# Second attention of a two-layer decoder: the low parts of the weights behind the copies of the transposed probabilities, and the last quarter's transposes behind nine products of the output projection

## The chip, the cores and the metric

The kernel runs on one core of a Trainium2 chip. The metric is the device time of one execution in microseconds (us). The kernel before takes 745.67 us, the median of three runs that lie between 745.35 and 746.33.

## The reference, cut to what matters

The program is a decoder trunk with two layers over 256 positions of 1024 numbers, all in float32. Layer 0 has a dilated attention, layer 1 a "forgetting" attention; behind each stands a SwiGLU feed-forward network. Each of the four is added to the residual stream and has an RMS norm ahead of it. The change lies in the second attention and the projection behind it:

```python
def forgetting_mixer(h, w_in, b_f, w_out):
    proj = h @ w_in                                  # 1024 -> 3*1024 + 16 gates
    q, k, v = ...                                    # 16 heads of 64
    c = lax.cumsum(log_sigmoid(proj[..., 3072:] + b_f), axis=1)
    def block(args):                                 # 128 queries at a time
        s = jnp.einsum('bihd,bjhd->bhij', qi, k) * HEAD_DIM ** -0.5
        s = s + ci[..., None] - ck[:, :, None, :]
        s = jnp.where(key_pos[None, :] <= qpos[:, None], s, NEG_INF)
        p = jax.nn.softmax(s, axis=-1)
        return jnp.einsum('bhij,bjhd->bihd', p, vf)
    return o @ w_out
```

## The kernel before, in words

**Products in three matmuls.** A float32 matrix is split into a high part (a copy in a shorter format) and a low part (the difference). Each product of two tiles is three matmuls: high by high, then two with one low part each (`mm3`, lines 198 to 208; a row of the profile shows the first as L202 and the other two as L207). Weights come from HBM as `raw` tiles of 128x1024 in five buffers, two of them to one piece of weights. For each, ScalarE (ACT) copies the high part `wh` (L79), then VectorE (DVE) subtracts for the low part `wl` (L83). When DVE has done so, the `raw` buffer is free, and the SyncE queue (SP) issues the transfer of the `raw` tile five places on. `weights` (line 149) asks for pieces two units ahead of their use.

**The second attention.** The loop over `b_units` (from line 934) takes one projection of 256 columns a round: for each quarter of the heads (four heads) first q, then k, and the v's of three quarters stand ahead of the loop. `due` holds the steps of the attention of a quarter that are hung into later rounds: the scores (`scores_b`) a round after k, the transposes of the probabilities (`trans_b`) one and a half rounds after the scores, between the two halves of that round's projection, and the products with v (`pv_b`) at the end of the same round, followed there by the next quarter's scores. So one round goes: half a projection, transposes of quarter n, the other half, `pv_b` of n, scores of n+1.

`scores_b` writes scores to four PSUM banks. DVE adds the bias and finds the maxima (L876), ACT takes exponentials (L878), DVE the reciprocals of the sums (L883), and both scale the probabilities `p` (L885 on ACT, L886 on DVE). `trans_b` transposes them on TensorE (PE, L298) into two banks `ps_tr` and one `ps_o`, and DVE copies the three to `pt` tiles (L303). `pv_b` needs these copies (L310); its results are split into `oth` (ACT) and `otl` (DVE), the operands of the output projection.

**The output projection.** `out_proj` (line 630) computes two halves of rows, t = 0 and 1. A product here is one of 16 for each t: n (two halves of the columns) by k (eight tiles of 128 rows of `ot`), three matmuls of 512 columns each. The last quarter gives k = 6 and 7, and its transposes and `pv_b` are still in `due` when `out_proj` begins. For t = 0 it makes the products of n = 0 over the first `done` k's, then the transposes, then what remains of these k's for n = 1, then `pv_b`, then the k's that are left.

**What sets the order.** The engines run in the order of their own instruction streams. The order is set by the code's order, by `first()` (a higher priority for the steps of an attention), and by `issue_after`, which puts an instruction behind another in the order. The list `behind` with `release` already does for the rounds 3 and 5 what the change does for others: it keeps low parts back until a given DVE instruction.

Of the kernel before, what the change touches and what calls it, by code (L numbers as in the profile page):

```python
# [19 lines left out]
KT = D // P  # L20
# [11 lines left out]
def trunk(ctx: ExitStack, tc: tile.TileContext, T, out):  # L32
# [10 lines left out]
    def first():  # L43

        return tc.high_priority(offset=300)

    def psum(tag):
        return ps.tile([P, 512], F32, tag=tag, name=f"ps_{tag}", bufs=2)
# [41 lines left out]
    def piece(key, todo=None):  # L90
        if key[0][:2] == "dn" and key[1] == LATE:
            wh, wl = (y.rearrange("p k c -> p (k c)") for y in fm_tile("ot", KT, 1))
        else:
            wh, wl = (wp.tile([P, WIDE], F32R, tag=y, name=y, bufs=4) for y in ("wh", "wl"))
        if key == GATED:
            wh, wl = (y.rearrange("p (k c) -> p k c", k=KT) for y in (wh, wl))
        for c in range(2):
            raw = wp.tile([P, 1024], F32, tag="raw", name="raw", bufs=5)
            u = slice(c * 1024, (c + 1) * 1024)
            nc.sync.dma_start(raw, T[key[0]][key[1]][:, u])  # L100
            view = lambda y, u=u: y[:, u]
            if key == GATED:
                raw = raw.rearrange("p (k c) -> p k c", c=256)
                view = lambda y, c=c: y[:, c * 4:c * 4 + 4, :256]
            cut = lambda after=None, hold=None, raw=raw, view=view: split((wh, wl), view, raw, False, after, hold)
            if todo is None:
                cut()
            else:
                todo.append(cut)
        if key == GATED:  # L110
            cut = lambda after=None, hold=None: split((wh, wl), lambda y: y[:, :, 256:], wf32, False, after, hold)
            todo.append(cut)
        return wh, wl
# [7 lines left out]
    def xt_tile():  # L121
        full = ap.tile([P, KT, 2, S], F32R, tag="xt", name="xt", bufs=1)
        x = XT((full[:, :, 0, :], full[:, :, 1, :]))
        x.full = full
        return x
# [27 lines left out]
    def weights(nm, i, after=None, ahead=AHEAD, hold=None):  # L153

        upto = order.index((nm, i)) + ahead
        while state["next"] <= min(upto, len(order) - 1):
            key = order[state["next"]]
            cuts = []
            ready[key] = piece(key, cuts)
            for cut in cuts:  # L160
                cut(after, hold)
            state["next"] += 1
        return ready.pop((nm, i))
# [46 lines left out]
    def both(pair, *idx):  # L210
        return tuple(x[idx] for x in pair)
# [43 lines left out]
    def v_tile(o=None, r=None):  # L255

        v = ap.tile([P, 512], F32, tag="v", name="v", bufs=7)
        with first():
            if r:
                for t in range(2):  # L260
                    s = slice(t * S, (t + 1) * S)
                    nc.scalar.activation(v[:, s], o[:, s], AF.Copy, scale=r[t])
            elif o is not None:
                nc.scalar.activation(v, o, AF.Copy)
        return v
# [24 lines left out]
    def masked(s, sc, mask):  # L290
        with first():
            nc.vector.scalar_tensor_tensor(s, sc, HD ** -0.5, mask, op0=ALU.mult, op1=ALU.add)

    def transposed(blocks, copy=nc.vector.tensor_copy, tag="tr", home="pt"):

        tr = psum(tag)
        for i, b in enumerate(blocks):
            nc.tensor.transpose(tr[:, i * P:(i + 1) * P], b, ident)  # L298
        n = len(blocks) * P
        bufs, cols = {"pt": (3, 512), "bias": (4, 6 * P)}[home]  # L300
        w = ap.tile([P, cols], F32, tag=home, name="pt", bufs=bufs)
        with first():
            copy(w[:, :n], tr[:, :n])  # L303
        return w

    def pv(o, v, kb, pr, w, n, start, stop):
# [21 lines left out]
    for i, c in enumerate(room):  # L328
        b = 1 + (i > 1)
        n = S + 512  # L330
# [17 lines left out]
    xt = xt_tile()  # L348
# [15 lines left out]
    part = [sums[:, :S], sums[:, S:512], sums[:, 512:], sqs[:, :512], sqs[:, 512:]]  # L364
# [8 lines left out]
    for k in range(KT):  # L373
        if k % 4 == 0:
            w = tuple(wp.tile([P, 2048], F32R, tag=y, name=y, bufs=4) for y in ("wh", "wl"))
# [49 lines left out]
    x = []  # L425

    ot = fm_tile("ot", KT, 1)
# [102 lines left out]
    due = {}  # L530
# [5 lines left out]
    for i, (hq, g, w) in enumerate(a_units):  # L536
# [3 lines left out]
        elif i:  # L540

            wt = weights("a_in", hq * 9 + g * 3 + w, read if i > 4 else None)
# [9 lines left out]
        if i in (24, 31):  # L552
            x.append(hrow("x"))
            t = len(x) - 1
            nc.sync.dma_start(x[t], T["x"][t * P:(t + 1) * P, :])
        if w < 2:
# [4 lines left out]
            if i == 2:  # L561
# [3 lines left out]
                wt = weights("a_in", 1, second)  # L565
# [61 lines left out]
                parts.append(sq(hn[:, s]))  # L627
        return hn, parts

    def out_proj(nm, ot, h, grow, done, banks):  # L630

        ws = [weights(nm, i) for i in range(4)]
        xt = xt_tile()
        res = []

        def part(t, acc, nk):
            last = None
            for n, k in nk:
                c = (k % 2) * D + n * 512
                last = mm3(acc[n], both(ot, ALL, k, slice(t * P, (t + 1) * P)),  # L640
                           both(ws[k // 2], ALL, slice(c, c + 512)), k == 0, k == KT - 1)
            return last

        def cols(ks):
            return [(n, k) for n in range(2) for k in ks]

        for t in range(2):
            acc = [psum(banks[t]) for _ in range(2)]
            if t == 0:

                nk = cols(range(done))
                last = part(t, acc, nk[:done])
                nk = nk[done:]
                per = -(-len(nk) // (len(due) - 1))
                for i in sorted(due):
                    with tc.issue_after(last.ins):
                        for fn, a in due[i]:
                            fn(*a)
                    last = part(t, acc, nk[:per]) or last
                    nk = nk[per:]  # L660
                due.clear()
                part(t, acc, nk)
                last = part(t, acc, cols(range(done, KT)))
            else:
                part(t, acc, cols(range(2)))
                with tc.issue_after(last.ins):
                    part(t, acc, cols(range(2, 6)))
                    norm_t(*res[0], grow, xt, 0)
                    part(t, acc, cols(range(6, KT)))
            res.append(residual(acc, h[t], f"h_{nm}{t}"))  # L670
        return res, xt
# [110 lines left out]
        return res  # L782

    g_f = load_grow(1)
    hs, xt = out_proj("a_out", ot, x, g_f, 6, ("sc", "mm"))
    causal = const("causal", [P, P])
    bf = cst.tile([P, NH], F32, name="bf")
    nc.sync.dma_start(bf, T["bf"].partition_broadcast(P))
# [9 lines left out]
    hs = ffn(0, hs, xt, g_f, mid)  # L798
    xt, g_b = nxt["xt"], nxt["g"]
# [26 lines left out]
    behind = []  # L826
# [27 lines left out]
    ot = fm_tile("ot", KT, 1)  # L854
# [79 lines left out]
    held = None  # L934
    for i, (hq, w) in enumerate(b_units):
        if i < 3:
            continue
        wt = weights("b_in", hq * 3 + w, behind if i in (3, 5) else None, hold=held)
        o = psum("mm")
        if w < 2:  # L940
            for c in range(2):
                proj_feat(xt, wt, o[:, c * S:(c + 1) * S], c)
                if c == 0:
                    for fn, a in due.pop(i - 0.5, ()):
                        fn(*a)
            if w == 0:

                for fn, a in due.pop(i, ()):
                    fn(*a)
            bq[hq][w] = ap.tile([P, 2, S], F32, tag=f"fm{w}", name=f"fb{w}", bufs=2)  # L950
            with first():
                held = nc.scalar.activation(bq[hq][w], o.rearrange("p (a b) -> p a b", a=2), AF.Copy,
                                            scale=(0.125, 1.0)[w])
            if w == 1:
                j = i + 1

                later(j, scores_b, hq)
                if hq < 2:
                    for pr in range(2):
                        later(j + 1, bias, hq + 2, pr)  # L960
                later(j + 1.5, trans_b, hq)
                for pr in range(2):
                    later(j + 2, pv_b, hq, pr)
        else:
            for t in range(2):
                proj_tok(xt, wt, o[:, t * S:(t + 1) * S], t)
                if t == 0:
                    for fn, a in due.pop(i - 0.5, ()):
                        fn(*a)
            bq[hq][w] = v_tile(o)  # L970
        for fn, a in due.pop(i, ()):
            fn(*a)
    g_f = load_grow(3)
    hs, xt = out_proj("b_out", ot, [h for h, _ in hs], g_f, 5, ("mm", "sc"))

    def finish(t, h, parts):
        r = rstd(parts)
# [10 lines left out]
    hs = ffn(1, hs, xt, g_f, mid)  # L988
    acc, h1 = hs[1]
# [3 lines left out]
    for o, (a, b) in zip(acc, ((0, 512), (512, 256), (768, 256))):  # L993
# [4 lines left out]
        else:  # L998
            parts.append(ap.tile([P, 1], F32, tag="ssq", name="ssq", bufs=8))
            last = nc.vector.scalar_tensor_tensor(psum("sc")[:, :b], hn[:, s], 1.0 / D, hn[:, s], op0=ALU.mult,  # L1000
                                                  op1=ALU.mult, accum_out=parts[-1])
# [104 lines left out]
```

## Time and profile before

| | |
|---|---|
| time, median of three runs | 745.67 us (745.35 to 746.33) |
| profiled execution: its own time / its span from first to last instruction | 749.27 us / 747.5 us |
| clock granted to PE, mean over the span | 0.994 |
| busy: PE / PE's weight loads | 737.5 us / 680.5 us |
| busy: DVE / ACT / POOL | 492.6 / 375.7 / 66.8 us |
| moved from and to HBM | 136.07 MB read, 1.07 MB written |

The page names engines by PE (matmul), PEld (its weight loads), DVE, ACT, POOL (GpSimd) and SPq (the queue of SyncE, which issues transfers). A row of a timeline has the start in us from the span's beginning, a length in us, the engine, the line of the kernel, the operation, what it writes and reads, a shape and a count; idle time ahead of it and what ended that stand in brackets. Where a count is above one, the row covers several instructions in succession. Lengths of matmuls overlap, since they are pipelined: what a matmul costs is read from start to start.

### The profile page before, as it was taken

What the parts mean: (1) busy time and instruction counts of PE and PEld (TensorE: products, weight loads), DVE (VectorE), ACT (ScalarE), POOL (GpSimd) and SP (SyncE); (2) the same over time, 40 slices, a digit from 0 to 9 for tenths busy, and PEclk for the clock granted to TensorE, in tenths of its full rate; (3) what the DMA queues carried; (4) which work ended last, traced back from release to release, by engine and by line L of the source; (5) the groups of instructions that cost most, each with busy time, mean ns of one, the idle gap of its engine ahead of it and who ended that gap; (6) DMA issues with size and microseconds to landing.
All of it is one profiled execution on the core that took longest, in us unless ns stands there. A gap on an engine that the chain in (4) does not pass through costs nothing.

```text
span 747.5 us, 14342 instructions
## 1 busy us (share of the span) xinstructions
PE 737.5 (99%) x5916; PEld 680.5 (91%) x5916; DVE 492.6 (66%) x768; ACT 375.7 (50%) x617; POOL 66.8 (9%) x98
## 2 busy tenths in 40 slices
PE   9999999999999999999999999999999999999996
PEld 7999989999988789999999988979789999999995
DVE  6997987787888575545455474686767545456533
ACT  7536437437436565344454453576555444444521
POOL 0600003005005000000000004211000000000001
PEclk9999999999999999999999999999999999999998
DMA  8865544644646267565667452874537665656601
GB/s 330 298 203 171 177 155 151 203 159 153 209 144 222 82 229 238 191 200 179 202 204 241 138 168 87 288 243 146 171 105 221 231 198 180 202 189 215 209 1 56
DMA packets 39441, 138.07 MB, mean 185 GB/s; under 512 B 4528, under 2 KB 5840, under 8 KB 39376
## 3 DMA queue, kind: packets, MB, share of 16 engines
q1 hardware_dynamic: 39232, 137.01, 55.3%
q8 instruction: 46, 0.75, 0.4%
q14 instruction: 19, 0.16, 0.1%
q10 hardware_dynamic: 144, 0.15, 0.1%
HBM read 136.07 MB, written 1.07 MB: 183 GB/s over the span
## 4 chain that ended last, share of the span: by engine, by line
PE 90%; ACT 3%; DMA 3%; DVE 2%; issue 1%; SPq 0%; POOL 0%; POOLq 0%; DVEq 0%; ACTq 0%
PE ps_mm L207 31%; PE ps_mm L202 16%; PE ps_tr L207 9%; PE ps_sc L207 8%; PE ps_o L207 7%; PE ps_tr L202 5%; PE ps_sc L202 4%; PE ps_o L202 4%; PE ps_o L310 2%; DMA raw<-in_b_in 2%; DVE wl L83 1%; DMA otl<-in_lead 1%; PE ps_tr L298 1%; ACT wh L79 1%; PE ps_sc L473 1%; ACT p L878 1%
## 5 line engine op out<-in xcount | busy, mean ns | idle before, releaser
L79 ACT ACTIVATE wh<-raw 128x1024 fp32r<-128x1024 f32 x236 | 243.2, 1055 | 240.4 <-PE ps_tr L207 66.5
L83 DVE TENSOR_TENSOR wl<-raw,wh 128x1024 fp32r<-128x1024 f32 x236 | 288.5, 1242 | 88.1 <-ACT wh L79 87.8
L202 PE MATMUL ps_mm<-xt,wh 128*128 128x256 f32 x816 | 228.2, 280 | 0.0
L207 PE MATMUL ps_mm<-xt,wl 128*128 128x256 f32 x816 | 226.8, 278 | 0.1
L207 PE MATMUL ps_mm<-xt,wh 128*128 128x256 f32 x816 | 226.6, 278 | 0.0
L202 PEld LDWEIGHTS ps_mm<-xt,wh 128*128 128x128 f32 x816 | 153.9, 189 | 1.8 <-issue 1.7
L207 PEld LDWEIGHTS ps_mm<-xt,wl 128*128 128x128 f32 x816 | 153.4, 188 | 0.5 <-DVE wl L83 0.5
L207 PEld LDWEIGHTS ps_mm<-xt,wh 128*128 128x128 f32 x816 | 153.4, 188 | 0.0
L207 PE MATMUL ps_tr<-xt,wl 128*128 128x256 f32 x304 | 83.8, 276 | 0.0
L207 PE MATMUL ps_tr<-xt,wh 128*128 128x256 f32 x304 | 83.8, 276 | 0.0
L202 PE MATMUL ps_tr<-xt,wh 128*128 128x256 f32 x304 | 83.6, 276 | 0.0
L702 DVE TENSOR_TENSOR sa<-ps_tr,sa 128x256 f32<-128x256 f32 x38 | 16.1, 424 | 73.9 <-PE ps_tr L207 73.8
L207 PEld LDWEIGHTS ps_tr<-xt,wh 128*128 128x128 f32 x304 | 57.1, 188 | 0.0
L207 PEld LDWEIGHTS ps_tr<-xt,wl 128*128 128x128 f32 x304 | 57.1, 188 | 0.0
L202 PEld LDWEIGHTS ps_tr<-xt,wh 128*128 128x128 f32 x304 | 56.9, 188 | 0.0
L284 POOL COPY v<-v 32x256 f32<-32x256 f32 x64 | 38.0, 594 | 176.1 <-ACT v L280 173.4
L202 PE MATMUL ps_mm<-wh,xt 128*128 128x512 f32 (+1 forms) x144 | 49.8, 346 | 0.0
L207 PE MATMUL ps_mm<-wl,xt 128*128 128x512 f32 (+1 forms) x149 | 49.1, 335 | 0.0
L207 PE MATMUL ps_mm<-wh,xt 128*128 128x512 f32 (+1 forms) x149 | 49.1, 335 | 0.0
L172 POOL TENSOR_SCALAR rs<-ssq 128x1 f32<-128x1 f32 x7 | 2.1, 303 | 422.8 <-ACT junk L181 422.8
L202 PE MATMUL ps_sc<-wh,ah 128*128 128x512 f32 x80 | 31.4, 392 | 0.0
L207 PE MATMUL ps_sc<-wl,ah 128*128 128x512 f32 (+1 forms) x82 | 31.3, 385 | 0.0
(230 smaller groups left out, 1103.3 us busy)
## 6 DMA issues: line engine op xcount, KB each, us to landing
raw<-in_gu SPq DMA_DIRECT2D x88, 512.0 KB, 4.8
raw<-in_a_in SPq DMA_DIRECT2D x68, 512.0 KB, 4.6
raw<-in_dn SPq DMA_DIRECT2D x44, 512.0 KB, 4.6
raw<-in_b_in SPq DMA_DIRECT2D x24, 512.0 KB, 4.7
raw<-in_a_out SPq DMA_DIRECT2D x8, 512.0 KB, 5.3
raw<-in_b_out SPq DMA_DIRECT2D x8, 512.0 KB, 4.9
bias<-sums SPq DMA_DIRECT2D x8, 384.0 KB, 6.1
grow<-in_norms SPq DMA_DIRECT2D x4, 512.0 KB, 5.9
```

The source lines that it names most:

```text
L79: a = nc.scalar.activation(view(hi), src, AF.Copy)
L83: return nc.vector.tensor_tensor(view(lo), src, view(hi).bitcast(F32), op=ALU.subtract)
L172: nc.gpsimd.tensor_scalar(m, s, rest, None, op0=ALU.add)
L202: nc.tensor.matmul(o, sh, mh, start=start, stop=False)
L207: last = nc.tensor.matmul(o[:, u], s, m[:, u], start=False, stop=end and u.stop == n)
L284: nc.gpsimd.tensor_copy(v[1 + a % 2][n:n + 32, a // 2 * S:a // 2 * S + S], by_t[a * 32:a * 32 + 32, t, g])
L298: nc.tensor.transpose(tr[:, i * P:(i + 1) * P], b, ident)
L310: nc.tensor.matmul(o[h * HD:(h + 1) * HD], v[:, c:c + HD], w(h), start=start, stop=stop)
L473: nc.tensor.matmul(sc[h][c, o:o + 64], q[HR[h], pr, qb * P + a * 32:qb * P + a * 32 + 32], k[HR[h], pr].rearrange("p (b n) -> p b n", b=2) ...
L702: nc.vector.tensor_tensor(a, u, sg, op=ALU.mult)
L878: nc.scalar.activation(s[:, u], s[:, u], AF.Exp, bias=nm[:, j:j + 1], scale=-1.0, accum_out=den[:, j:j + 1])
```

## The change

Two things are changed. In rounds where transposes are due (7, 9 and 11), the low parts of the weights that the round asks for are kept in a list `lows` and are put behind the last copy of the transposed probabilities (`copied["last"]`) in DVE's order. And `out_proj` has two numbers in the place of one: `ks`, the k's that are ready ahead of the last quarter (6 in both attentions; for the second it was 5), and `done`, the products ahead of the first step that is due (9 for the second attention, where it was 5). For the first attention both are 6, which is what was there.

```diff
+    copied = {}
+
     def transposed(blocks, copy=nc.vector.tensor_copy, tag="tr", home="pt"):
...
-            copy(w[:, :n], tr[:, :n])
+            copied["last"] = copy(w[:, :n], tr[:, :n])
...
-    def out_proj(nm, ot, h, grow, done, banks):
+    def out_proj(nm, ot, h, grow, ks, done, banks):
...
-                nk = cols(range(done))
+                nk = cols(range(ks))
                 last = part(t, acc, nk[:done])
                 nk = nk[done:]
...
-                last = part(t, acc, cols(range(done, KT)))
+                last = part(t, acc, cols(range(ks, KT)))
...
-        wt = weights("b_in", hq * 3 + w, behind if i in (3, 5) else None, hold=held)
+        lows = [] if any(fn is trans_b for fn, _ in due.get(i - 0.5, ())) else None
+        wt = weights("b_in", hq * 3 + w, behind if i in (3, 5) else lows, hold=held)
...
                     for fn, a in due.pop(i - 0.5, ()):
                         fn(*a)
+                    for low in lows or ():
+                        low(copied["last"])
...
-    hs, xt = out_proj("b_out", ot, [h for h, _ in hs], g_f, 5, ("mm", "sc"))
+    hs, xt = out_proj("b_out", ot, [h for h, _ in hs], g_f, 6, 9, ("mm", "sc"))
```

On DVE, at the first quarter's transposes, the order before is this (`wl_5564` and `wl_5631` are low parts of two pieces of the input projection, `pt` the copies, `otl` the low part of the first quarter's result):

```order
L83 TENSOR_TENSOR wl_5564<-raw_5567,wh_5563 128x1024
L83 TENSOR_TENSOR wl_5631<-raw_5632,wh_5630 128x1024
L83 TENSOR_TENSOR wl_5631<-raw_5634,wh_5630 128x1024
L303 COPY pt_5670<-ps_tr_5665 128x512
L303 COPY pt_5677<-ps_tr_5672 128x512
L303 COPY pt_5684<-ps_o_5679 128x512
L83 TENSOR_TENSOR wl_5775<-raw_5776,wh_5774 128x1024
L83 TENSOR_TENSOR otl_5128<-ps_o_5710,oth_5127 128x256
```

With the change, the same place on DVE has this order:

```order
L83 TENSOR_TENSOR wl_5564<-raw_5567,wh_5563 128x1024
L305 COPY pt_5668<-ps_tr_5663 128x512
L305 COPY pt_5675<-ps_tr_5670 128x512
L305 COPY pt_5682<-ps_o_5677 128x512
L83 TENSOR_TENSOR wl_5631<-raw_5632,wh_5630 128x1024
L83 TENSOR_TENSOR wl_5631<-raw_5634,wh_5630 128x1024
L83 TENSOR_TENSOR wl_5775<-raw_5776,wh_5774 128x1024
L83 TENSOR_TENSOR otl_5128<-ps_o_5710,oth_5127 128x256
```

The two halves of `wl_5631`, which the round two units later uses, have moved behind the three copies; one low part still stands ahead of them. On DVE at the third quarter's transposes, the order before is this (`wl_6047`, `wl_6193` and `wl_6203` belong to the output projection):

```order
L83 TENSOR_TENSOR wl_6047<-raw_6048,wh_6046 128x1024
L83 TENSOR_TENSOR wl_6047<-raw_6050,wh_6046 128x1024
L303 COPY pt_6086<-ps_tr_6081 128x512
L303 COPY pt_6093<-ps_tr_6088 128x512
L303 COPY pt_6100<-ps_o_6095 128x512
L83 TENSOR_TENSOR wl_6193<-raw_6194,wh_6192 128x1024
L83 TENSOR_TENSOR wl_6193<-raw_6196,wh_6192 128x1024
L83 TENSOR_TENSOR wl_6203<-raw_6204,wh_6202 128x1024
L83 TENSOR_TENSOR otl_5128<-ps_o_6128,oth_5127 128x256
```

With the change it is this:

```order
L305 COPY pt_6084<-ps_tr_6079 128x512
L305 COPY pt_6091<-ps_tr_6086 128x512
L305 COPY pt_6098<-ps_o_6093 128x512
L83 TENSOR_TENSOR wl_6047<-raw_6048,wh_6046 128x1024
L83 TENSOR_TENSOR wl_6047<-raw_6050,wh_6046 128x1024
L83 TENSOR_TENSOR wl_6193<-raw_6194,wh_6192 128x1024
L83 TENSOR_TENSOR wl_6193<-raw_6196,wh_6192 128x1024
L83 TENSOR_TENSOR otl_5128<-ps_o_6128,oth_5127 128x256
```

The two halves of `wl_6047`, and with them the release of `raw_6048` and `raw_6050`, have moved behind the copies, and `wl_6203` of `raw_6204` has moved further back, behind the next reciprocal. The other half of `wl_6203`, of `raw_6206`, now stands ahead of the last reciprocal, where before it stood ahead of an earlier scaling. At the second quarter the two halves `wl_5842` go behind the copies in the same way. ACT, POOL and SP keep their orders. On PE, within the output projection, the order before is this, from the fifth product's last matmul on (`ps_mm` the sums of t = 0):

```order
L207 MATMUL ps_mm<-wh,otl 128x512
L298 MATMUL ps_tr<-ident,p 128x128
L202 MATMUL ps_mm<-wh,oth 128x512
L298 MATMUL ps_tr<-ident,p 128x128 x5
L207 MATMUL ps_mm<-wl,oth 128x512
L207 MATMUL ps_mm<-wh,otl 128x512
L298 MATMUL ps_o<-ident,p 128x128
L202 MATMUL ps_mm<-wh,oth 128x512
L207 MATMUL ps_mm<-wl,oth 128x512
L298 MATMUL ps_tr<-ident,p 128x128 x2
L298 MATMUL ps_o<-ident,p 128x128 x3
L207 MATMUL ps_mm<-wh,otl 128x512
```

With the change it is this, from the ninth product's last matmul on:

```order
L207 MATMUL ps_mm<-wh,otl 128x512
L300 MATMUL ps_tr<-ident,p 128x128 x8
L300 MATMUL ps_o<-ident,p 128x128 x4
L202 MATMUL ps_mm<-wh,oth 128x512
L207 MATMUL ps_mm<-wl,oth 128x512
```

The twelve transposes stand in one block behind nine products, where before they were strewn between the matmuls of the sixth and seventh product. Three products follow them ahead of `pv_b`, and four follow `pv_b`, where it was six.

More of the change, by code (lines that the diff above doesn't have):

```diff
@@ L784, in trunk @@
     g_f = load_grow(1)
-    hs, xt = out_proj("a_out", ot, x, g_f, 6, ("sc", "mm"))
+    hs, xt = out_proj("a_out", ot, x, g_f, 6, 6, ("sc", "mm"))
     causal = const("causal", [P, P])
@@ L969, in trunk @@
                         fn(*a)
+                    for low in lows or ():
+                        low(copied["last"])
             bq[hq][w] = v_tile(o)
```

## The prediction

> **What bounds the kernel now.** First the page's busy times and the table of waits, cut to PE:
>
> ```profile
> PE 737.5 (99%) x5916; PEld 680.5 (91%) x5916; DVE 492.6 (66%) x768; ACT 375.7 (50%) x617; POOL 66.8 (9%) x98
> ...
> PE ps_o L310 <- DVE pt L303: 1.8, 2, 1.6
> ```
>
> PE is busy for 737.5 of 747.5 us, so a change that removes no matmul can only gain where PE waits or runs slowly, and a delay on another engine costs only where PE comes to wait for it. The second row is nearly all the waiting that PE has: the products with v wait for the copies of the transposed probabilities, 1.6 us at the longest. PE's timeline has the place, in the first quarter:
>
> ```profile
> 489.45 1.16 PE L298 MATMUL ps_tr<-ident,p 128*128 128x128 f32 x8
> ...
> 490.80 0.37 PE L202 MATMUL ps_mm<-xt,wh 128*128 128x256 f32 x1
> ...
> 493.51 0.28 PE L207 MATMUL ps_mm<-xt,wl 128*128 128x256 f32 x1
> 495.38 1.03 PE L310 MATMUL ps_o<-pt,v 128*64 128x256 f32 x8 [1.59 <-DVE pt L303]
> 496.57 1.44 PE L310 MATMUL ps_o<-pt,v 128*64 128x256 f32 x8 [0.16 <-DVE pt L303]
> 497.94 1.65 PE L864 MATMUL ps_sc<-fb,fb 64*128 64x128 f32 x8
> ...
> 500.50 0.38 PE L202 MATMUL ps_mm<-xt,wh 128*128 128x256 f32 x1
> ```
>
> The same stretch of the second quarter, which has the same instructions and no wait:
>
> ```profile
> 513.02 0.28 PE L207 MATMUL ps_mm<-xt,wl 128*128 128x256 f32 x1
> 513.23 1.52 PE L310 MATMUL ps_o<-pt,v 128*64 128x256 f32 x16
> 514.68 0.93 PE L864 MATMUL ps_sc<-fb,fb 64*128 64x128 f32 x8
> ...
> 516.19 0.38 PE L202 MATMUL ps_mm<-xt,wh 128*128 128x256 f32 x1
> ```
>
> From the last matmul of the projection to the first of the next, the second quarter needs 516.19 - 513.02 = 3.17 us, the first 500.50 - 493.51 = 6.99. The difference, 3.82, is more than the wait of 1.59. The rest is in the products, which get their copies one at a time, and in the scores: 500.50 - 497.94 = 2.56 us for the same sixteen matmuls that take 516.19 - 514.68 = 1.51. Half-microsecond windows (the fourth number from the end, ahead of the DMA share, is the granted clock) say why:
>
> ```profile
> 496.50:497.00 0.50, 0.43 (x4) 0.26 (x6) 0.50 (x2) 0.34 (x1) 0.00 (x0) 0.72 0.81 320
> 497.00:497.50 0.50, 0.50 (x6) 0.31 (x4) 0.50 (x1) 0.00 (x0) 0.00 (x0) 0.50 0.97 279
> ...
> 500.00:500.50 0.50, 0.50 (x6) 0.15 (x3) 0.50 (x5) 0.44 (x3) 0.00 (x0) 0.86 1.01 311
> ```
>
> After the wait the granted clock is 0.50 from about 496.7 to 500.1, some 3.4 us, which costs up to 1.7 of the 3.82. The Trainium skill, "TensorE: Matmul & The Clock Gate", Part 1 (the HAM clock gate), says that the clock falls to half after an idle window of about 3.4 us. The measured length of the slow stretch agrees with that window; the 1.59 us of idleness ahead of it is shorter than the rule asks for.
>
> Why the copies came late is in DVE's timeline of that place (its second row is the first alone of the three that the row above it covers):
>
> ```profile
> 490.13 4.58 DVE L83 TENSOR_TENSOR wl<-raw,wh 128x1024 fp32r<-128x1024 f32 x3
> 490.13 2.32 DVE L83 TENSOR_TENSOR wl<-raw,wh 128x1024 fp32r<-128x1024 f32 x1
> ...
> 494.64 1.27 DVE L303 COPY pt<-ps_tr 128x512 f32<-128x512 f32 x2
> 495.84 0.67 DVE L303 COPY pt<-ps_o 128x512 f32<-128x512 f32 x1
> ...
> 497.57 0.41 DVE L83 TENSOR_TENSOR otl<-ps_o,oth 128x256 fp32r<-128x256 f32 x1
> ...
> 499.73 0.29 DVE L876 CUSTOM_DVE_ANT_0 p<-ps_sc,bias 128x128 f32<-128x128 f32 x1 [0.84 <-PE ps_sc L864]
> ```
>
> The transposes were through at about 491, and three low parts kept DVE until 494.64.
>
> **First part: the low parts behind the copies.** Nothing is added or removed; two subtractions change places with three copies, once a quarter. In the first quarter the copies now follow one low part, which ends at 490.13 + 2.32 = 492.45. The three take 494.64 to 496.51, that is 1.87, so they end at 494.32; the first is there at about 493.1, the second at 493.7. PE comes to the products at 493.51 + 0.21 = 493.72 (the step of the second quarter), needs the third copy only for its second half, 0.73 later, at 494.45, and finds all three. The wait, the piecemeal products and, if it comes from the wait, the half clock are gone: 3.8 us. What is late next is DVE. Its two low parts and the one that followed already (0.5 x (4.58 - 2.32) = 1.13 each) end at 494.2 + 3 x 1.13 = 497.6, as in the row of `otl` before; the two `otl` take some 0.7, and the second quarter's L876 starts at 498.3, 1.4 earlier than at 499.73, while PE is 3.8 earlier. Who waits for that is PE at the second transposes:
>
> ```profile
> 504.51 0.70 ACT L885 ACTIVATE p<-p,c_b 128x128 f32<-128x128 f32 x2 [0.24 <-DVE c_b L883]
> ...
> 509.09 1.04 PE L298 MATMUL ps_tr<-ident,p 128*128 128x128 f32 x8
> ```
>
> The probabilities are ready at 505.2, and PE came at 509.1, 3.9 later. Now they are ready at 503.8, and PE comes at 505.3: a cover of 1.5 us is left, so I take nothing. The matmuls that use the moved `wl_5631` come two rounds later, from about 502.3, against 496.5 for its end: nothing. From there the second quarter stands to PE as before, and in it and the third no PE wait is there to be removed: nothing gained.
>
> **Second part: nine products ahead of the transposes.** PE's rows of the output projection, t = 0: its first matmul, the fifth product's last, the first transpose, `pv_b`, the first matmul after it, and the first of t = 1:
>
> ```profile
> 531.68 0.50 PE L202 MATMUL ps_mm<-wh,oth 128*128 128x512 f32 x1
> ...
> 534.99 0.39 PE L207 MATMUL ps_mm<-wh,otl 128*128 128x512 f32 x1
> 535.62 0.33 PE L298 MATMUL ps_tr<-ident,p 128*128 128x128 f32 x1 [0.24 <-ACT p L885]
> ...
> 541.01 1.52 PE L310 MATMUL ps_o<-pt,v 128*64 128x256 f32 x16
> 542.47 0.50 PE L202 MATMUL ps_mm<-wh,oth 128*128 128x512 f32 x1
> ...
> 546.68 0.39 PE L202 MATMUL ps_sc<-wh,oth 128*128 128x512 f32 x1
> ```
>
> All of it takes 546.68 - 531.68 = 15.00. The 18 matmuls after `pv_b` take (546.68 - 542.47)/18 = 0.234 each; 48 of them are 11.23. The transposes in one block are 490.80 - 489.45 = 1.35, `pv_b` 542.47 - 541.01 = 1.46. Sum 14.04: about 0.95 us goes to waits for probabilities that are scaled while PE stands at them, and this is what the second part can gain. It gains it if all is ready after nine products, 27 x 0.236 = 6.4 us after the first matmul (0.236 is 3.31/14 from the first two rows). I count from that matmul, zero being 531.68 before. These rows set the time of the probabilities, ACT's last cast of weights, first exponential and last scaling, then the third transposes on PE and the low part after which the cast's `raw` is fetched, with its issue on SP:
>
> ```profile
> 530.79 1.07 ACT L79 ACTIVATE wh<-raw 128x1024 fp32r<-128x1024 f32 x1
> 532.53 0.40 ACT L878 ACTIVATE p<-p,nm_b 128x128 f32<-128x128 f32 x1 [0.67 <-DVE nm_b L876]
> ...
> 536.99 0.40 ACT L885 ACTIVATE p<-p,c_b 128x128 f32<-128x128 f32 x1 [0.24 <-DVE c_b L883]
> ...
> 524.48 1.04 PE L298 MATMUL ps_tr<-ident,p 128*128 128x128 f32 x8
> ...
> 523.66 1.23 DVE L83 TENSOR_TENSOR wl<-raw,wh 128x1024 fp32r<-128x1024 f32 x1 [1.54 <-ACT wh L79]
> ...
> 524.91 0.33 SPq L100 DMA_DIRECT2D raw<-in_b_out  x1
> ```
>
> On DVE the third quarter's copies start 0.65 after the transposes' -7.2, take 1.8, and the four low parts behind them end at -4.75 + 4 x 1.14 = -0.2; with the two `otl` L876 starts at +0.5, as before (532.20). But the cast of `raw_6206` stands ahead of the exponentials in ACT's order, and `raw_6206` takes the buffer that the first half of `wl_6047` frees. Before, that was at 524.91, -6.8; now the half ends at -3.5. With T for the time to landing, the cast starts at T - 3.5, ends at T - 2.45, and the exponentials start there or at +0.85. From first exponential to the last pair of probabilities are 536.99 + 0.70 - 532.53 = 5.2, and 0.5 more since a low part now stands ahead of the last reciprocal: 5.7. DVE's share of them, which PE needs first, is there at 5.5. PE begins the transposes at 6.4, and comes to the first that needs the last pair six transposes on, 0.65 later, at 7.05. So there is no wait if T - 2.45 + 5.5 is below 7.05, T below 4.0; above that PE waits T - 4.0. T is what decides. The trace has these for such transfers: the one just ahead of it (issued at 520.29), the very one (524.91), and one issued at 473.32 amid bias transfers:
>
> ```profile
> raw<-in_b_out SPq DMA_DIRECT2D x1, 512.0 KB, 3.6
> ...
> raw<-in_b_out SPq DMA_DIRECT2D x1, 512.0 KB, 5.1
> ...
> DMA to landing us min/median/max: 8.9/8.9/8.9
> ```
>
> The second row is odd, since nothing was in flight ahead of it; I take the first, that of an undisturbed transfer, and no wait. After the transposes, three products (2.1 us) cover the copies. `pv_b` is followed at once by k = 6, where before k = 5 stood between; its `oth` came 0.9 after `pv_b`'s start and PE is at k = 6 after 1.46: covered. The later transfers of the feed-forward weights are issued 1 to 3 us later against PE and are used some 25 us after: nothing.
>
> **Sum.** 3.8 + 0.9 = 4.7 us. The profiled execution, 749.27 us (span 747.5), would come to 744.6. It is 3.6 above the median of the runs; waits of PE carry over one to one, so 745.67 - 4.7 = 741.0.
>
> **Rivals.** (1) The late `raw` costs the second part: T = 5.1, PE waits 1.1 to 1.2 at the transposes, 742.2. For it, the very row; against it, its neighbour. The Trainium skill, "TensorE: Matmul & The Clock Gate", on engine queue depths, says that ScalarE and VectorE are strict FIFO. By that rule the exponentials cannot pass the waiting cast, as the trace's order of ACT shows too. (2) The half clock isn't the wait's: the clock's window falls there anyway, 1.7 of the 3.8 stay, 742.7. Against it: the fall comes right behind the one long wait that PE has. The skill's rule quoted above would have it so, since the idleness was too short for it. (3) DVE gets late for the second transposes: if the three low parts take 2.32 each, as the one at 490.13 did, instead of 1.14, they end 3.5 later, the cover of 1.5 is spent, PE waits 2.0: 743.0. Against it: the others there took 1.13. (4) Slower: the same queue as in (1), with T = 8.9. PE waits 4.9 at the last transposes, and the half clock that followed 1.6 us of waiting follows this too, 1.7: 741.0 + 6.6 = 747.6. This decides from T = 8.4 on (741.0 + 4.4 + 1.7 = 745.67 + 0.2%); from T = 5.4 with the half clock it is no change. Against it: the 8.9 had bias transfers around it, and none is due then. That the change does not do what it says is excluded by the orders shown.
>
> **Chances.** Forecast 0.48; (1) 0.25; (2) 0.10; (3) 0.10; no change by (4)'s milder form 0.04; slower 0.03. About 0.2%, 1.5 us, can be told from no change. Faster is 0.93. The range goes from 741.0 less half the 1.0 us by which the runs differ, 740.4, to (3) and as much above, 743.5.
>
> **What would show it.** Right: no wait of L310 (now L312) for DVE; 3.2 us from the projection's last matmul to the next first one in the first quarter; granted clock 1.00 there; 14.0 to 14.2 us for t = 0 of the output projection. Rival (1) shows as ACT's cast L79 waiting for `raw<-in_b_out` right ahead of the exponentials, and PE's L300 for DVE or ACT. (3) shows as PE waiting at the second transposes. The prediction is wrong if the first quarter's stretch stays above 4 us, or if new PE waits sum to over 2 us.

## The result, and the profile after

The changed kernel takes 742.89 us, the median of six runs (742.58 to 743.51); the kernel before, run beside it, 745.89 (six runs, 745.23 to 748.07). The ratio is 0.9958, with a 95% interval of 0.9944 to 0.9971: 3.0 us faster, between 2.2 and 4.2. The forecast was 741.0 with a range of 740.4 to 743.5. Among the executions of the kernel before that were run beside the experiments, one took 2918.8 us; no ratio below counts it.

The profiled execution of the changed kernel took 742.58 us, with a span of 740.8 and a granted clock of 0.998. Its busy times:

```profile
PE 732.5 (99%) x5916; PEld 678.0 (92%) x5916; DVE 490.6 (66%) x768; ACT 375.5 (51%) x617; POOL 67.0 (9%) x98
```

Its table of waits has no row of PE waiting for `pt` any more. PE's timeline at the first quarter, from the last matmul of the projection to the first of the next:

```profile
491.86 0.28 PE L207 MATMUL ps_mm<-xt,wl 128*128 128x256 f32 x1
492.07 1.52 PE L312 MATMUL ps_o<-pt,v 128*64 128x256 f32 x16
493.52 0.93 PE L866 MATMUL ps_sc<-fb,fb 64*128 64x128 f32 x8
...
495.03 0.38 PE L202 MATMUL ps_mm<-xt,wh 128*128 128x256 f32 x1
```

The stretch is 495.03 - 491.86 = 3.17 us, all sixteen products with v stand in one row, and the scores take 1.51 as in the second quarter. It was 6.99. DVE's timeline of the same place, down to the last scaling ahead of the second transposes:

```profile
488.27 1.22 DVE L83 TENSOR_TENSOR wl<-raw,wh 128x1024 fp32r<-128x1024 f32 x1
489.40 1.28 DVE L305 COPY pt<-ps_tr 128x512 f32<-128x512 f32 x2
490.60 0.68 DVE L305 COPY pt<-ps_o 128x512 f32<-128x512 f32 x1
491.20 2.35 DVE L83 TENSOR_TENSOR wl<-raw,wh 128x1024 fp32r<-128x1024 f32 x2
493.75 1.23 DVE L83 TENSOR_TENSOR wl<-raw,wh 128x1024 fp32r<-128x1024 f32 x1 [0.20 <-ACT wh L79]
...
500.34 0.62 DVE L888 TENSOR_SCALAR p<-p,c_b 128x256 f32<-128x256 f32 x2
```

The copies end at 491.28, ahead of PE's need at 492.07. The last probabilities of the second quarter are ready at about 501.0, and PE comes for them here:

```profile
503.32 1.04 PE L300 MATMUL ps_tr<-ident,p 128*128 128x128 f32 x8
```

So a cover of 2.3 us is left there. The output projection, t = 0, on PE: first matmul, the ninth product's last, the transposes, `pv_b`, the first matmul behind it, the first of t = 1:

```profile
525.92 0.50 PE L202 MATMUL ps_mm<-wh,oth 128*128 128x512 f32 x1
...
531.95 0.39 PE L207 MATMUL ps_mm<-wh,otl 128*128 128x512 f32 x1
532.18 1.03 PE L300 MATMUL ps_tr<-ident,p 128*128 128x128 f32 x8
...
535.67 1.52 PE L312 MATMUL ps_o<-pt,v 128*64 128x256 f32 x16
...
539.97 0.39 PE L202 MATMUL ps_sc<-wh,oth 128*128 128x512 f32 x1
```

It takes 539.97 - 525.92 = 14.05 us; it was 15.00. The chain behind these transposes, on ACT, DVE and SP (the last cast of weights, the first exponential, the last scalings, the issue of the cast's `raw`), and that transfer's time to landing:

```profile
526.23 1.06 ACT L79 ACTIVATE wh<-raw 128x1024 fp32r<-128x1024 f32 x1 [1.08 <-DMA raw<-in_b_out]
527.20 0.39 ACT L880 ACTIVATE p<-p,nm_b 128x128 f32<-128x128 f32 x1
...
532.15 0.70 ACT L887 ACTIVATE p<-p,c_b 128x128 f32<-128x128 f32 x2 [0.76 <-DVE c_b L885]
...
532.16 0.62 DVE L888 TENSOR_SCALAR p<-p,c_b 128x256 f32<-128x256 f32 x2
...
522.41 0.33 SPq L100 DMA_DIRECT2D raw<-in_b_out  x1
...
DMA to landing us min/median/max: 3.8/3.8/3.8
```

The cast does wait for its transfer, 1.08 us, and the exponentials queue behind it. The last pair is scaled at about 532.8, and PE comes to it some six transposes after 532.18, at 532.83: no wait, and no slack either.

The two spans differ by 747.5 - 740.8 = 6.7 us, more than the medians by far. In the changed places the traces differ by 3.82 (the stretch) and 0.95 (the projection); about 1.5 was there already at 431 us, ahead of anything that the change touches. Most of that 1.5 arises in the first 105 us: the 901st matmul starts at 104.1 us in the profile of before and at 102.8 in that of the change. The clock is 1.00 in all stretches there, and what held the matmuls up wasn't traced, nor was the 0.4 that is left.

### The profile page after: what moved, and what is told of

It is laid out like the page before. It is cut to its first block, busy times and chain, and to the rows that moved or that the text cites. A ratio compares the mean times of both kernels' runs of the same rounds, so it can differ in the third digit from the quotient of the medians.

```text
span 740.8 us, 14341 instructions
## 1 busy us (share of the span) xinstructions
PE 732.5 (99%) x5916; PEld 678.0 (92%) x5916; DVE 490.6 (66%) x768; ACT 375.5 (51%) x617; POOL 67.0 (9%) x98
## 4 chain that ended last, share of the span: by engine, by line
PE 96%; ACT 1%; DMA 1%; DVE 1%; issue 0%; SPq 0%; POOL 0%; POOLq 0%; DVEq 0%; ACTq 0%
PE ps_mm L207 34%; PE ps_mm L202 17%; PE ps_tr L207 9%; PE ps_sc L207 8%; PE ps_o L207 7%; PE ps_tr L202 5%; PE ps_sc L202 4%; PE ps_o L202 4%; PE ps_o L312 2%; PE ps_tr L300 1%; DMA otl<-in_lead 1%; PE ps_sc L475 1%; PE ps_tr L195 1%; PE ps_o L300 1%; PE ps_sc L457 0%; PE ps_sc L866 0%
```

## The experiments

The forecast took 3.8 us for the first part from one execution, in which the clock fell to half behind the wait. The theory under test, A in the expectations: the half clock comes from the wait, but only in some executions. A usual execution of the kernel before has the wait without it, and loses less there than the profiled one did. The rivals: the half clock belongs to every execution, and part of the gain was lost somewhere in the changed kernel; or the half clock has nothing to do with the wait.

**The kernel before, unchanged, with another profile.**

> The kernel before, unchanged, run as if it were a change. What has to be explained: the change gave 3.0 us in the median of the runs, while the stretch that it touches is some 5 us shorter in the two profiled executions. Theory A (the half clock behind the first quarter's wait comes in some executions only; the wait is in all): a mean granted clock of 0.996 or more in most of these runs, and a profiled execution where the first quarter's stretch from the last projection matmul to the next first one takes about 5.3 us (3.2 and a wait and piecemeal products of 2.1), against 6.99 in the profile before. Theory B (the half clock is there every time, and the change loses elsewhere in most runs): the stretch takes 6.9 us again, clock about 0.994. Time 745 to 747 by both.

It took 745.61 us (11 runs, 744.73 to 746.05), ratio 0.9997 (0.9989 to 1.0006). The profiled execution was one of 745.94 us. Its stretch at the first quarter, then the row of its table of waits (total, times, longest):

```profile
492.02 0.28 PE L207 MATMUL ps_mm<-xt,wl 128*128 128x256 f32 x1
493.37 1.04 PE L310 MATMUL ps_o<-pt,v 128*64 128x256 f32 x8 [1.08 <-DVE pt L303]
494.57 0.87 PE L310 MATMUL ps_o<-pt,v 128*64 128x256 f32 x8 [0.16 <-DVE pt L303]
495.37 0.93 PE L864 MATMUL ps_sc<-fb,fb 64*128 64x128 f32 x8
...
496.88 0.38 PE L202 MATMUL ps_mm<-xt,wh 128*128 128x256 f32 x1
```

```profile
PE ps_o L310 <- DVE pt L303: 1.2, 2, 1.1
```

The wait and the piecemeal products are there, but the scores take 496.88 - 495.37 = 1.51 us, the same as everywhere, and the granted clock is 1.00 in every half microsecond around it. The stretch is 4.86 us: what the first part can gain over it is 4.86 - 3.17 = 1.69, not 3.82. All eleven runs had a clock of 0.997 to 0.999; the profiled execution of the prediction had 0.994. A has what it expected, except that the stretch is shorter than its 5.3, since the wait is shorter too.

**The first part alone.** The low parts move, and the output projection keeps five products ahead of the transposes:

```diff
-    hs, xt = out_proj("b_out", ot, [h for h, _ in hs], g_f, 6, 9, ("mm", "sc"))
+    hs, xt = out_proj("b_out", ot, [h for h, _ in hs], g_f, 5, 5, ("mm", "sc"))
```

> The first part alone: low parts behind the copies in all three rounds, output projection as before (5 products ahead of the transposes). Theory A: 2.1 us less than before in the median, and 3.8 in executions of before with the half clock. Theory B: 3.8 less. By both the output projection can lose up to 1 us, since the raw tile that the last cast needs comes later and the transposes still stand behind five products: the probabilities are there 6.5 to 7 us after the first product, as before.

It took 743.61 us (9 runs, 743.16 to 744.43), ratio 0.9976 (0.9966 to 0.9985): 2.0 us. All three stretches are 3.17 us, t = 0 of the projection is 14.8, and the waits of PE that are left, beside two at the program's start, are those at its transposes:

```profile
PE ps_tr L300 <- ACT p L887: 0.4, 1, 0.4
PE ps_tr L300 <- DVE p L888: 0.2, 1, 0.2
```

By the traces this is 1.69 + 0.2 = 1.9.

**The second part alone.** The numbers 6 and 9 stay, and no low part moves:

```diff
-        lows = [] if any(fn is trans_b for fn, _ in due.get(i - 0.5, ())) else None
+        lows = None
```

> The second part alone: nine products ahead of the last quarter's transposes, low parts where they were. Theories A and B agree on 0.9 us less than before: t = 0 of the output projection takes 14.05 us in place of 15.0, with the first quarter's wait of 1.6 us unchanged.

It took 744.55 us (11 runs, 743.77 to 745.69), ratio 0.9987 (0.9978 to 0.9996): 1.05 us. The stretch is 4.76 with the wait in it, and t = 0 is 14.05, which makes 0.1 + 0.95. The two parts alone add up to 3.05, the whole change within the noise: no shared or spoilt gain shows.

**Low parts moved in the first quarter's round alone**, and the projection as before:

```diff
-        lows = [] if any(fn is trans_b for fn, _ in due.get(i - 0.5, ())) else None
+        lows = [] if i == 7 else None
...
-    hs, xt = out_proj("b_out", ot, [h for h, _ in hs], g_f, 6, 9, ("mm", "sc"))
+    hs, xt = out_proj("b_out", ot, [h for h, _ in hs], g_f, 5, 5, ("mm", "sc"))
```

> The low parts behind the copies in the first quarter's round alone, output projection as before. Theory A: 2.1 us less than before (no loss in the output projection, which stays at 15.0). Theory B: 3.8 us less. If the second and the third quarter's moves gave or cost something, this run differs from the one with all three by that.

It took 744.51 us (11 runs, 743.81 to 745.27), ratio 0.9987 (0.9978 to 0.9996): 1.1 us, half of what the move in all rounds gives and half of what A expected. The first stretch is 3.17, but the second has become 3.56, and its timeline shows a new wait:

```profile
507.53 0.88 PE L312 MATMUL ps_o<-pt,v 128*64 128x256 f32 x8
508.56 0.87 PE L312 MATMUL ps_o<-pt,v 128*64 128x256 f32 x8 [0.16 <-DVE pt L305]
```

PE now comes 1.7 us earlier, DVE gained less, and the copies of the second quarter, still behind two low parts, are late in their turn. In this trace the two low parts also took 3.86 us, beside additions on POOL, where `again`, the kernel before in its second profile, has 2.67; the two causes aren't separated. Of the 0.9 us by which this run is behind the first part alone, the traces show 0.4 here and 0.2 in the projection. So the later moves gain nothing over the kernel before, but they keep what the first has gained; an experiment below shows that the third quarter's isn't needed for it.

**A longer wait: the first quarter's copies made twice**, in the kernel before. Nothing is left out; each copy is written a second time:

```diff
-            copy(w[:, :n], tr[:, :n])
+            for _ in range(2 if bq[0].get("again") else 1):
+                copy(w[:, :n], tr[:, :n])
...
+        bq[0]["again"] = hq == 0
```

> The kernel before, with each of the first quarter's three copies of transposed probabilities made twice: the last copy ends 1.8 us later, so PE's wait there grows from about 1.3 to 1.9 (first copy) and 3.1 us (last). Nothing of the computation is left out. Theory A (the half clock is set off by the wait, if it is long enough where the clock's monitor looks): the stretch of the first quarter grows from 4.86 by 1.8 to 6.7 us without the half clock and to 8.4 with it, and the half clock now shows in more executions than before: mean granted clock at or below 0.996 in a good part of them, median 1.8 to 3.5 us above before. Theory B' (the half clock in the first profile of before was chance and has nothing to do with this wait): 1.8 us above before, clock 0.997 to 0.999 in all executions.

The runs fall into groups. Two of the ten took 746.46 and 746.47 us, at a clock of 0.999; four 748.61 to 749.12, at 0.996 or 0.997 but for one at 0.994; four 750.02 to 751.41, at 0.992 or 0.993. The median is 749.04, ratio 1.0045 (1.0031 to 1.0059), while the runs of the kernel before beside it all had 0.997 to 0.999. The profiled execution was one of the two at full clock. Its stretch:

```profile
491.93 0.28 PE L207 MATMUL ps_mm<-xt,wl 128*128 128x256 f32 x1
493.90 1.04 PE L311 MATMUL ps_o<-pt,v 128*64 128x256 f32 x8 [1.70 <-DVE pt L304]
...
495.92 0.87 PE L311 MATMUL ps_o<-pt,v 128*64 128x256 f32 x8 [0.56 <-DVE pt L304]
...
498.00 0.39 PE L202 MATMUL ps_mm<-xt,wh 128*128 128x256 f32 x1
```

That is 6.07 us, 1.2 more than with single copies, at full clock. It isn't the 6.7 that was expected, for two things that the edit doesn't ask for: the three low parts ahead of the copies took 3.48 us here, where `again` has 4.58 (the last section says why), and four matmuls of the scores have moved between the two halves of the products. So the longer wait by itself is worth about 1 us, and the executions that take 2 to 5 us more have a lower clock. Where in the program the clock fell, this trace couldn't show.

**The same kernel for another profile.**

> The same kernel as with two sets of copies, for one more look: its profile there was one of the two executions of ten without the loss of clock. Theory A: with a chance of 8 in 10 this execution shows a clock of 0.997 or less, a time of 748.6 or more, and windows with 0.50 right behind the first quarter's wait, 3.4 us or a little more of them; the stretch is then 7.5 to 8 in place of 6.07. Rival: the half clock, if there is any, lies at another place.

This execution took 750.08 us at a clock of 0.993. PE's rows of the products, then half-microsecond windows (the granted clock is the third number from the end):

```profile
494.75 1.04 PE L311 MATMUL ps_o<-pt,v 128*64 128x256 f32 x8 [2.11 <-DVE pt L304]
...
496.76 1.55 PE L311 MATMUL ps_o<-pt,v 128*64 128x256 f32 x8 [0.32 <-DVE pt L304]
```

```profile
495.00:495.50 0.50, 0.50 (x6) 0.16 (x4) 0.50 (x2) 0.00 (x0) 0.00 (x0) 1.00 1.09 279
495.50:496.00 0.50, 0.50 (x6) 0.33 (x6) 0.47 (x2) 0.17 (x1) 0.00 (x0) 0.83 0.69 188
...
502.50:503.00 0.50, 0.50 (x6) 0.50 (x5) 0.50 (x1) 0.50 (x4) 0.00 (x0) 0.84 1.03 301
```

The clock is 0.50 from about 495.8 to 502.7, about 1 us after the wait ended, and nowhere else in the program but at its very end. That is 6.8 us at half, which can cost up to 3.4. The execution took 750.08 - 746.47 = 3.6 us more than the one of the same kernel at full clock, and the wait is longer too: from the projection's last matmul (492.36) to the first product are 2.39 us, against 1.97. The stretch of 8.32 us is a little over the 7.5 to 8 expected.

**The copies made three times.**

> The kernel before with the first quarter's three copies made three times (nothing is left out). Each further set of copies cost 1.2 us of stretch in the run with two sets (6.07 against 4.86, no half clock), so the stretch becomes 7.3 without half clock. Theory A (the half clock comes from the wait): with a wait of some 3 us the half clock is there in at least as many executions as with two sets (8 of 10), about 3.4 us of it cost up to 1.7, median 748.0 + 1.7 to 748.0 + 4, so 749.7 to 752; its profile shows 0.50 directly behind the products' wait in the first quarter and nowhere else. Rival (the loss of clock in the run with two sets lies elsewhere, or has no relation to the wait): median 748.0, clocks of 0.997 to 0.999 in most runs, or half clock at another place than behind this wait.

It took 750.10 us (4 runs, 749.54 to 750.81), ratio 1.0054 (1.0035 to 1.0073). All four lost clock, two at 0.992 and two at 0.995 and 0.996. The profiled one has 0.50 from 495.25 to 502.08, and nowhere else but at the end. Its wait is 2.81 us long and ends at 495.72, so that the clock fell 0.5 us before PE went on.

With single copies the clock fell in few executions (the one of the prediction, and one of seven beside these two experiments, 747.80 us at 0.995; another long one, 748.42 us, had 0.997, which decides nothing), with two sets in nine of eleven (one of them, 749.12 us, by its time alone, since its clock was 0.997), with three in all four, and each of the three profiles that caught it has it within this wait or at most 1.4 us behind its end. That the half clock comes from the wait, and isn't in every execution, is shown. What decides between the executions is in the last section.

**The change without its move in the third quarter's round.** Its low parts stand ahead of the copies again, so that the `raw` of the last cast is fetched earlier:

```diff
-        lows = [] if any(fn is trans_b for fn, _ in due.get(i - 0.5, ())) else None
+        lows = [] if i in (7, 9) else None
```

> The change, but with the third quarter's low parts ahead of the copies, as in the kernel before; rounds 7 and 9 and the nine products as in the change. It takes away the late release of the raw tile that ACT's last cast ahead of the exponentials waits for (1.08 us in the profile of the change). If that wait costs PE nothing (forecast: a landing time below 4.0 us): time as with the change, within 0.3 us, t = 0 of the output projection 14.05 us, and no wait of that cast. If in most executions the tile lands later than in the profile (rival 1): up to 1.1 us faster than the change.

It took 742.97 us (5 runs, 742.13 to 743.40), ratio 0.9962 (0.995 to 0.9975), the same as the change. The cast no longer waits for its transfer, and yet t = 0 takes 14.09. So the late `raw` of the change costs nothing that these runs can tell, and its move in the third round gains nothing.

**Seven and twelve products ahead of the transposes**, in place of nine; the edit is that number.

> The change with seven products ahead of the last quarter's transposes in place of nine. PE comes to the transposes 1.4 us earlier, ahead of the probabilities (6.3 us after the first product in the change): t = 0 of the output projection takes 14.6 to 15.1 us in place of 14.05, with waits for ACT and DVE at the transposes. If the probabilities were not the limit: 14.05.

Seven: 743.22 us, one execution. t = 0 is 14.84 us, the transposes stand between matmuls again, and PE waits:

```profile
PE ps_tr L300 <- DVE p L888: 0.5, 1, 0.5
```

> The change with all twelve products ahead of the transposes, none behind them ahead of the products with v. The copies take 2.5 us from the first transpose's start to the last copy's end, and the transposes 1.35: PE waits for copies, 0.5 to 1.0 us in all, t = 0 takes 14.5 to 15.0 us. If three products there were not needed as cover: 14.05.

Twelve: 743.85 us, one execution. No product is left between transposes and `pv_b`, which waits for the copies instead; PE filled in three matmuls of t = 1:

```profile
536.20 0.65 PE L312 MATMUL ps_o<-pt,v 128*64 128x256 f32 x4
536.78 0.50 PE L202 MATMUL ps_sc<-wh,oth 128*128 128x512 f32 x1
537.22 0.44 PE L312 MATMUL ps_o<-pt,v 128*64 128x128 f32 x4
...
538.25 0.87 PE L312 MATMUL ps_o<-pt,v 128*64 128x256 f32 x8
539.05 0.50 PE L202 MATMUL ps_mm<-wh,oth 128*128 128x512 f32 x1
```

From 536.20 to 539.05 are 2.85 us; three matmuls at 0.23 off, 2.15 for a `pv_b` that takes 1.46 when its operands are there. So nine lies between a wait for probabilities and a wait for copies. By the times alone the three counts are not told apart: single executions of 743.22 and 743.85 stand against runs of 742.58 to 743.51.

## Why the prediction was right, and what was off in it

**The first part: mechanism right, size off.** The forecast was 4.7 us and 3.0 came. The wait, the piecemeal products and the half clock are gone, as foreseen, and the stretch is the 3.17 us of the second quarter. The term of 3.8 is too large by 2.1: in a usual execution of the kernel before the stretch is 4.86, and the part alone gained 2.0 us. The step that failed is "waits of PE carry over one to one, so 745.67 - 4.7 = 741.0". Waits do carry over, but a half clock that is in one execution and not in the three that make the median doesn't. The sign stood in the prediction itself: the profiled execution was 3.6 us above the median. Of these, 6.99 - 4.86 = 2.13 are the stretch, and 1.5 lie earlier. Of the 2.13, some 0.5 is a longer wait (from the last matmul to the first product 495.38 - 493.51 = 1.87, against 493.37 - 492.02 = 1.35), and the other 1.6 is what 3.4 us at half clock cost. Taken with the stretch of a usual execution, the same steps give 745.67 - 1.69 - 0.95 = 743.0, against 742.89 measured. That 742.89 lies within the range is luck: the range went up to 743.5 for the sake of rival (3), which didn't come.

Three small things in the working are off without bearing on it. The lower end, 741.0 less half of 1.0, is 740.5. The granted clock is the third number from the end of a window's row, not the fourth; the values named are the clock's. And the row of 1.8 us isn't nearly all of PE's waiting: 0.9 at the program's start and 0.2 at the last transposes are in the same table.

The prediction set its row against the Trainium skill, "TensorE: Matmul & The Clock Gate", Part 1, by which an idle window of about 3.4 us sets the clock to half. The runs have the clock fall at waits of 1.6, 2.1 and 2.8 us, all shorter than that. Here the measurement decides. The same part of the Trainium skill also says that this window runs freely, so that the point of a change of clock depends on where in it a matmul lands; the traces agree, as the last section shows.

**DVE next late: right, with more cover.** The cover at the second transposes was put at 1.5 us and is 2.3: the low part ahead of the copies took 1.22, not the 2.32 of the trace before, so that all of DVE's steps behind it came 1.1 earlier. That DVE gains less than PE showed in the experiment with the first round alone, at another place than the prediction named: with the later low parts left in place, 0.4 us went at the second `pv_b`.

**The second part: right.** 14.05 us against 14.04 forecast, and 1.05 measured alone against 0.9. The condition T below 4.0 held by a little: T was 3.8, and the scaling ended where PE came for it.

**The rivals.** (1) The late `raw` did make the cast wait, 1.08 us, but PE didn't; without it the time is the same. (2) Its price, 742.7, came nearest to the measured time, but for a reason that isn't the case: the half clock was the wait's, and none is left in the changed kernel. It was simply not in the usual execution before. (3) and (4) did not come: all three low parts behind the copies took 1.13 to 1.23, and T was far from 8.4.

## What to carry to other kernels

Compare the time of the profiled execution with the median before a stretch of it is priced: where it is longer, look for half-clock windows, and take the price of the stretch without them. When one late step on a busy engine is put right, look at the same step in the next rounds, since the engine ahead gains less than the one that waited for it; moving all of them keeps the gain. A long wait of PE costs its length for certain. In these traces half clock came on top, worth up to 1.7 or 3.4 us, where PE stood idle for 1.75 us or more of one 3.41 us step of the grid described below, and not where it stood idle for up to 1.67.

## What the runs showed of the hardware

The half clock keeps to a grid of 3.41 us. In each of the three traces that caught it, the clock's changes lie whole steps of 3.413 us apart: 496.72, 500.14 and, at the program's end, 742.48 in the profile of the prediction (1 step, then 71), 495.83, 502.66 and 745.00 with two sets of copies (2, then 71), 495.25, 502.08 and 744.43 with three (2, then 71). So the half clock comes in lengths, 3.4 us in the first and 6.8 in the others. Runs of one kernel fall into groups (746.5, about 749, 750 to 751.4), which would fit no, one and two steps; of that kernel only the first and the last kind were profiled.

The grid also tells why one execution loses clock and another doesn't. The fall at the program's end places it in the traces where the clock stayed at 1.00. Below are steps around the wait (the number behind the comma is PE's busy time): the profile of the prediction, two sets of copies where the clock fell, and three sets with the step that follows; then two sets where it didn't fall (two steps, and one near the program's end), and `again`:

```profile
493.31:496.72 3.41, 1.66 (x15) 0.82 (x15) 3.41 (x6) 1.80 (x3) 0.00 (x0) 1.00 0.67 219
...
492.42:495.83 3.41, 1.30 (x12) 0.53 (x13) 3.41 (x6) 1.54 (x2) 0.00 (x0) 1.00 0.92 297
...
491.84:495.25 3.41, 1.06 (x8) 0.74 (x6) 3.41 (x6) 1.54 (x2) 0.00 (x0) 1.00 0.74 245
495.25:498.67 3.42, 2.95 (x12) 1.59 (x14) 2.32 (x5) 0.44 (x2) 0.00 (x0) 0.50 0.42 166
```

```profile
490.31:493.72 3.41, 1.90 (x17) 1.70 (x15) 3.41 (x5) 1.51 (x3) 0.00 (x0) 1.00 0.80 243
493.72:497.14 3.42, 2.68 (x24) 1.67 (x26) 3.38 (x6) 1.71 (x4) 0.00 (x0) 1.00 0.65 223
...
736.07:739.48 3.41, 1.74 (x14) 1.50 (x12) 3.30 (x10) 1.12 (x4) 0.62 (x2) 1.00 0.40 154
...
492.04:495.45 3.41, 2.17 (x21) 1.01 (x19) 3.41 (x5) 1.93 (x3) 0.00 (x0) 1.00 0.95 303
```

In all twelve traces of this case the clock fell at the end of every step with PE busy for 1.66 us or less, and of none with 1.74 or more. Half a step is 1.71. With two sets of copies at full clock, 2.2 us of idleness were split over two steps, 1.5 and 0.7; in `again` there were only 1.24. In the profile of the prediction there were 1.75, all in one step. The clock rose again behind the first step in which PE was busy all through: the first one in the profile of the prediction, the second in the other two, whose first had 3.09 and 2.95 us. This is a regularity of twelve traces, read with modelled ends of matmuls; no run set a wait against the grid on purpose.

A subtraction on DVE and an addition on POOL slow each other, and the one that starts second pays. In the kernel before, POOL's addition began first and took 1.30 us, and DVE's low part right behind it more than twice its 1.2:

```profile
488.06 1.30 POOL L851 TENSOR_TENSOR bias<-bias,causal 128x512 f32<-128x512 f32 x1 [0.99 <-DVE p L886]
...
488.14 4.58 DVE L83 TENSOR_TENSOR wl<-raw,wh 128x1024 fp32r<-128x1024 f32 x3
```

(4.58 for three, where three undisturbed ones take 3.5.) In the changed kernel DVE was first by 0.02 us: its low part took 1.22, and POOL's addition 2.36:

```profile
488.29 2.36 POOL L853 TENSOR_TENSOR bias<-bias,causal 128x512 f32<-128x512 f32 x1 [2.29 <-DMA bias<-sums]
```

The Trainium skill, "SBUF — State Buffer", "SBUF: two separate sides", says that the port pair these two share is locked for a whole instruction by whichever starts first; both rows agree. Which of the two comes first differs between the twelve traces: at this place POOL did in seven, and in four of these it was still at it when DVE began. That costs DVE about 1.1 us, but it doesn't decide the wait alone. With the second part alone DVE was first, yet its next low part waited 0.65 us for its high part on ACT, the last two took 2.72 us, and PE waited 0.97. And with the low parts moved in the first round alone POOL came first, the low part ahead of the copies took 2.30 us, and the stretch was 3.17 all the same.
